# Weight buffers of a streaming encoder layer: high and low parts 64 bytes apart, four buffers at four places modulo 256 bytes

## The chip, the core and the metric

The kernel runs on one core of one Trainium2 chip. The metric is device time in microseconds of the whole program, one launch. Before the change it is 2326.92 us, the median of 3 runs (2326.52 to 2327.61). Experiments further down compare each kernel with the one before the change on the same chip.

## The reference

The reference is one step of a hybrid encoder layer on two sets of frames, 512 of a new stream and 64 of a running one, 576 in all, with 2048 channels, in float32:

```
hn = rmsnorm(x, g_norm1)
q, k, v, gb, gc, hc = split(hn @ w_in)              # 6 x 1024 columns
o_attn = stick_breaking(rmsnorm(q), rmsnorm(k), v)  # 8 heads x 128; the 64 frames also see 512 cached ones
o_conv = gb * conv3(gc * hc)                        # causal, 3 taps
x = x + concat(rmsnorm(o_attn), rmsnorm(o_conv)) @ w_out      # 2048 x 2048
h2 = rmsnorm(x, g_norm2)
x = x + (silu(h2 @ w_gate) * (h2 @ w_up)) @ w_down  # 2048 x 5632, twice, and 5632 x 2048
```

It returns the new x, the new keys and values, and the state of the convolution. Nearly all of the arithmetic is in the five weight matrices w_in, w_out, w_gate, w_up and w_down.

## The kernel before, in words

**Layout.** Channels lie on the 128 partitions, frames on the free axis. The 576 frames are handled as two halves of 288 (HALF). Every product is a series of matmuls in which 128 x 128 weights are loaded into the array and 288 frames are streamed past them.

**Two parts for each number.** A float32 operand is split in two: a high part, which ScalarE makes by a cast to the matmul's format (float32r), and a low part, the rest, which VectorE makes by a subtraction (lines 291 and 292, 228 and 231, 784 and 787, 1484 and 1487). A product then takes three matmuls for each 128 channels: high weights by high frames, low weights by high frames, high weights by low frames. In the text these three are a triple. Weights are split as they arrive from memory; frames are split once and stay in SBUF, high part and low part behind each other in a tile of 2 x 288 numbers, so the low part begins 1,152 bytes behind the high one.

**Units.** Most of the work is done in units of a seven-product scheme (Strassen's, in the form with few sums): a unit has two by two blocks of weights and two by two blocks of frames, seven products instead of eight, numbered 1 to 7 in the code. A product of a gate or up unit has NP = 8 weight blocks of 128 x 128, so 8 x 3 = 24 matmuls, all into one PSUM tile (psy, psw or psx). There are 44 gate and up units and 37 pieces of 8 down units (line 2028), units of the same kind for five pairs of input columns (line 1162), and for the convolution's columns and the attention half of w_out (line 1515). The first columns of w_in and the convolution half of w_out are done without the scheme, by `product` (line 282).

**Weight buffers.** The pool wpool holds one raw tile of 16,384 bytes of each partition (raw_a), into which SyncE's DMAs bring weights, and two tags, whi and wlo, with two buffers each of 8,192 bytes. As the program is laid out, raw_a begins at byte 2,816 of each partition and the four buffers at 19,200, 27,392, 35,584 and 43,776, all of them at 0 modulo 256. The weights of line 282 use one whi and one wlo buffer, high part in the one and low part in the other. A unit's product uses one buffer alone, whl: the tile is [2, NP, 128], its first 4,096 bytes are the high part and the rest the low part, and products take the tags in turn, so that the four buffers go round. The tiles `lpad` (32 bytes, behind wpool, rpool and tmp on the left side) and `rpad` (224 bytes, first on the right) bring the tiles that follow to multiples of 256; streamed frames begin at 0 (high part) or 128 (low part) modulo 256.

**Order.** TensorE's instructions stand in the order in which the code writes them. A unit's products follow a written list (`order`, and `horder` and `corder` in the earlier stages); `prepare` (from line 1981), `unit_prepare` and `conv_prepare` split the weights of a product four places ahead of the one that runs. So a buffer's cast waits until the product that used it before has run, and its contents are needed some three products later. Splitting a gate or up product's weights is one ScalarE cast and one VectorE subtraction of 128 x 1024. VectorE also makes the sums of weight blocks that the seven-product scheme needs, and most of the work behind the products.

Of the kernel before, what the change touches and what calls it, by code (L numbers as in the profile page):

```python
# [11 lines left out]
F32R = mybir.dt.float32r  # L12
# [4 lines left out]
P = 128  # L17
# [17 lines left out]
NP = KD // 2  # L35
# [32 lines left out]
def down_calls():  # L68

    done, calls, gone = [0] * DC, [], 0  # L70
    for d, a, b in DOWN:
        assert done[d] == a and b <= gone + SLOTS
        done[d] = b
        calls.append([p + SLOTS for p in range(gone, min(done)) if p + SLOTS < NFP])
        gone = min(done)
    assert gone == NFP
    return calls


class Pipeline:  # L80


    def __init__(self):
        self.now, self.seq, self.heap = 0, 0, []
# [24 lines left out]
def tile_hybrid_stream_step(  # L109
# [19 lines left out]
    wpool = ctx.enter_context(tc.tile_pool(name="wpool", bufs=2, side="left"))  # L129
# [45 lines left out]
    ready = []  # L175
    raw_tile = {"A": wpool.tile([P, 2, 2048], F32, tag="raw", name="raw_a", bufs=1)}

    def weight_raw(i):
        src, nk, ncol = specs[i]
        raw = raw_tile["A"][:, 0 if len(EARLY) <= i < first_out else i % 2, : nk * ncol]  # L180
        return raw, raw.rearrange("p (k c) -> p k c", k=nk), src

    def weight_split(i):
        nk, ncol = specs[i][1:]
        hi = wpool.tile([P, 2048], F32R, tag="whi", name=f"whi{i}")[:, : nk * ncol]
        lo = wpool.tile([P, 2048], F32R, tag="wlo", name=f"wlo{i}")[:, : nk * ncol]
        ready.append((hi.rearrange("p (k c) -> p k c", k=nk), lo.rearrange("p (k c) -> p k c", k=nk)))
        return hi, lo

# [272 lines left out]
    with tc.manual_schedule(engines={mybir.EngineType.Activation, mybir.EngineType.DVE, mybir.EngineType.SP}):  # L462
        raw, raw3, src = weight_raw(0)
        raws[0] = raw
        hi, lo = weight_split(0)
# [317 lines left out]
    def cast(hi, src):  # L783
        nc.scalar.copy(out=hi, in_=src)

    def low(lo, src, hi):
        nc.vector.tensor_tensor(out=lo, in0=src, in1=hi.bitcast(F32), op=ALU.subtract)
# [314 lines left out]
    bt = {}  # L1102
    hfree, hregion, hst, hoper = [], {}, {}, {}
# [4 lines left out]
    def call_blocks(gone):  # L1108
        hfree.extend(gone)
        while hwanted and hfree:  # L1110
            n, c, s = hwanted.pop(0)
            q = hfree.pop(0)
            v = bt["g"] if q == 4 else raw_tile["A"][:, q // 2, q % 2 * 1024 : (q % 2 + 1) * 1024]
            v = v.rearrange("p (j c) -> p j c", c=P)
            c0 = UNIT_COLS[n][c][0] * AW + UNIT_COLS[n][c][1] * P
            nc.sync.dma_start(out=v, in_=w_in[:, c0 : c0 + P].rearrange("(j s p) c -> s p j c", s=2, p=P)[s])
            hregion[n, c, s] = q, v

    def unit_prepare(n, p_):
        st, tt = hst.setdefault(n, {"gone": []}), nc.vector.tensor_tensor  # L1120
        gone, own = st["gone"], bt["own"]
        first_sum = p_ in (6, 7) and 6 not in gone and 7 not in gone

        def raw(c, s):
            return hregion[n, c, s][1]

        if first_sum:
            tt(out=raw(1, 0), in0=raw(1, 0), in1=raw(0, 0), op=ALU.subtract)
            if p_ == 6:
                tt(out=own, in0=raw(1, 0), in1=raw(1, 1), op=ALU.add)  # L1130
        src = own if p_ in (3, 6) else raw(*{1: (0, 0), 2: (0, 1), 4: (1, 1), 5: (1, 0), 7: (1, 0)}[p_])
        bt["turn"] = bt.get("turn", 0) + 1
        whl = hoper[n, p_] = wpool.tile([P, 2, NP, P], F32R, tag=("whi", "wlo")[bt["turn"] % 2], name="whl")
        cast(whl[:, 0], src)
        if first_sum and p_ == 7:
            tt(out=own, in0=raw(1, 0), in1=raw(1, 1), op=ALU.add)
        yield 2
        low(whl[:, 1], src, whl[:, 0])
        gone.append(p_)
        if p_ in (6, 7) and not first_sum:  # L1140
            yield 1
            tt(out=raw(1, 0), in0=own, in1=raw(0, 0), op=ALU.add)
            tt(out=own, in0=raw(0, 1), in1=own, op=ALU.subtract)
        free = {4: [(1, 1)], 5: [(1, 0)]}.get(p_, [])
        if p_ in (2, 6, 7) and all(q in gone for q in (2, 6, 7)):
            free = [(0, 0), (0, 1)]
        call_blocks([hregion.pop((n, c, s))[0] for c, s in free])
# [144 lines left out]
    for q in (2, 3):  # L1292
        pipe.spawn(unit_prepare(*horder[q]), 3 * (q - 2))
# [134 lines left out]
    cturn = [0]  # L1428
# [26 lines left out]
    def conv_prepare(n, p_):  # L1455

        st, tt, m = cst.setdefault(n, {"left": 7, "gone": []}), nc.vector.tensor_tensor, NP if n < NCU else NH // 2
        gone, early = st["gone"], n < NCU  # L1460
        first_sum = early and p_ in (6, 7) and 6 not in gone and 7 not in gone
        if p_ == 1:
            _, st["a11"], st["a12"] = cregion[n, 0]
            st["at"] = {p: st[s] for p, s in ((1, "a11"), (2, "a12"))}
        at = st["at"]
        if first_sum or not early and p_ == 6:
            _, st["a21"], st["a22"] = cregion[n, 1]
            a11, a12, a21, a22 = (st[s] for s in ("a11", "a12", "a21", "a22"))
            own = bt["s1"] if early else bt["s1"][:, n % 2 * m : (n % 2 + 1) * m]
            at.update({3: own, 4: a22, 5: a21, 6: own, 7: a21} if early else {3: a12, 4: a22, 5: own, 6: a11, 7: a21})  # L1470
            if not early:
                tt(out=own, in0=a21, in1=a22, op=ALU.add)
            tt(out=a21, in0=a21, in1=a11, op=ALU.subtract)
            if not early:
                tt(out=a11, in0=own, in1=a11, op=ALU.subtract)
            elif p_ == 6:
                tt(out=own, in0=a21, in1=a22, op=ALU.add)
        if not early and p_ == 3:
            tt(out=at[3], in0=at[3], in1=at[6], op=ALU.subtract)
        src = at[p_]  # L1480
        cturn[0] += 1
        whl = wpool.tile([P, 2, NP, P], F32R, tag=("whi", "wlo")[cturn[0] % 2], name="whl")[:, :, :m]
        coper[n, p_] = whl
        nc.scalar.copy(out=whl[:, 0], in_=src)
        if first_sum and p_ == 7:
            tt(out=at[6], in0=at[7], in1=at[4], op=ALU.add)
        tt(out=whl[:, 1], in0=src, in1=whl[:, 0].bitcast(F32), op=ALU.subtract)
        gone.append(p_)
        if early and p_ in (6, 7) and not first_sum:
            tt(out=at[5], in0=at[6], in1=st["a11"], op=ALU.add)  # L1490
            tt(out=at[3], in0=st["a12"], in1=at[6], op=ALU.subtract)
        if p_ == 4 or (p_ in (2, 6, 7) and all(q in gone for q in (2, 6, 7)) if early else p_ == 3):
            c = int(p_ == 4)
            q = cregion.pop((n, c))[0]
            if n < NCU or (n, 1 - c) not in cregion:
                call_columns([q])
# [167 lines left out]
    for k_, (n, p_) in enumerate(corder):  # L1664
# [9 lines left out]
        if n == NCU - 1 and p_ in (6, 7, 4):  # L1674
            q = {6: 1, 7: 2, 4: 3}[p_]
            t = bt["pool"].tile([P, NH, 2, HALF], F32R, tag=f"t{q}", name=f"forms{q}")
# [286 lines left out]
    slot_turn = [0]  # L1963
# [17 lines left out]
    def prepare(n, p_):  # L1981

        st = unit.setdefault(n, {"summed": -1})
        m = UNITS[n][3]
        if p_ == 1:
            st["a11"], st["a12"] = (region[n, 0][0][:, :, q, :] for q in range(2))
        if p_ == 7 and n == 0:
            one_sum(n)
            one_sum(n)
        if p_ == 6:  # L1990
            while st["summed"] != 6:
                one_sum(n)
        if p_ == 3:
            while st["summed"] != 3:
                one_sum(n)
        src = {1: "a11", 2: "a12", 3: "a12", 4: "a22", 5: "s1", 6: "a11", 7: "a21"}[p_]
        slot_turn[0] += 1
        whl = wpool.tile([P, 2, NP, P], F32R, tag=("whi", "wlo")[slot_turn[0] % 2], name="whl")[:, :, :m]
        split(whl[:, 0], whl[:, 1], st[src])
        operand[n, p_] = whl  # L2000
        if n >= NGU:

            if p_ == 1:
                summing.append(n)
            if summing and p_ != 2:
                k = summing[0]
                if unit[k]["summed"] != 6 or p_ == 6:
                    one_sum(k)
                if unit[k]["summed"] == 3:
                    summing.pop(0)  # L2010
        if p_ in (3, 4):
            st["gone"] = st.get("gone", 0) + 1
            if n < NGU:
                load_columns(region.pop((n, p_ - 3))[1])
            elif st["gone"] == 2:
                load_columns(region.pop((n, 0))[1])
# [104 lines left out]
    for d, v in visits.items():  # L2121
        n = next(a for a, b in zip(v, v[1:]) if a >= NGU + 10 and b >= a + 4)
# [6 lines left out]
    turn = [0]  # L2129
# [252 lines left out]
```

## Time and profile before

| | |
|---|---|
| median of 3 runs | 2326.92 us |
| the profiled execution | 2329.04 us |
| its span in the profile | 2327.3 us |
| mean granted TensorE clock | 0.999 |
| instructions in the span | 43,744 |
| matmuls, and weight loads | 17,437 each |
| DMA traffic | 402.54 MB, mean 173 GB/s |

The profile is one execution of the program. Times are in microseconds, and ns where it is said. PE is TensorE's matmuls, PEld its weight loads, which overlap them; DVE is VectorE, ACT ScalarE, POOL GpSimd, SP SyncE. Matmuls are pipelined and their ends are modelled, so the length that a row gives for one matmul (some 294 ns) is longer than the distance from one matmul's start to the next; the distance is read from starts, or from a count in a stretch without idle time. The chain is the work that ended last, followed back from the end of the program; a piece of it is a start, a length, an engine, a tile, a line and a count. In a row of a group stand the line, engine, operation, the tile written and the tiles read, partitions x elements and the count; then the busy time, the mean ns of one, and the engine's idle time before them with what ended it.

### The profile page before, as it was taken

The page shows a single profiled execution, that of the slowest core. Times are in us where ns is not written, and L with a number is a line of the kernel's source. Part 1 is how long each engine was busy: PE and PEld are TensorE (multiplying, and loading weights), DVE is VectorE, ACT ScalarE, POOL GpSimd, SP SyncE. Part 2 cuts the span into 40 slices and gives each one's busy share as a digit, 9 for nine tenths or more (in the row PEclk, how much of TensorE's full clock was granted, in tenths as well). Part 3 has the DMA queues.
Part 4 walks back from the last instruction along what each step waited for, and adds up shares of the span by engine and source line. Part 5 has one row for each costly group of instructions (what it writes and reads, how often), then busy time and mean ns, then how long its engine had stood idle before and what let it go on. Part 6 is the DMA issues. An engine that isn't in the chain of part 4 may idle for free.

```text
span 2327.3 us, 43744 instructions
## 1 busy us (share of the span) xinstructions
PE 2317.9 (100%) x17437; PEld 2310.7 (99%) x17437; DVE 1919.4 (82%) x2853; ACT 1161.8 (50%) x2016; POOL 284.8 (12%) x394
## 2 busy tenths in 40 slices
PE   9999999999999999999999999999999999999999
PEld 9999999999999999999999999999999999999999
DVE  8977887888877899888888888888888777887886
ACT  7535887444445564444444444444444444444444
POOL 2002343111111220000000000000000001431121
PEclk9999999999999999999999999999999999999999
DMA  8776564953389454444444444344354936886653
GB/s 277 212 207 169 151 156 107 335 182 117 111 271 238 150 175 145 155 145 134 155 130 149 141 138 154 122 153 151 116 160 138 358 114 219 218 238 198 194 133 103
DMA packets 584869, 402.54 MB, mean 173 GB/s; under 512 B 91870, under 2 KB 571864, under 8 KB 584664
## 3 DMA queue, kind: packets, MB, share of 16 engines
q1 hardware_dynamic: 574136, 378.56, 52.3%
q0 software_dynamic: 10160, 20.94, 4.0%
q8 instruction: 136, 2.23, 0.4%
q14 instruction: 69, 0.57, 0.1%
q10 hardware_dynamic: 368, 0.24, 0.0%
HBM read 303.53 MB, written 96.16 MB: 172 GB/s over the span
## 4 chain that ended last, share of the span: by engine, by line
PE 92%; DVE 3%; DMA 3%; SPq 1%; issue 1%; ACT 0%; ACTq 0%; DVEq 0%
PE psy L2028 36%; PE psw L2028 18%; PE psx L2028 9%; PE psy L1515 6%; PE pj L282 6%; PE pjo L282 4%; PE psw L1515 3%; PE psy L1162 3%; PE psx L1515 2%; PE psw L1162 1%; DMA raw_a<-in_w_in_dram 1%; PE psx L1162 1%; DMA form_dram<-hf 1%; PE po L1048 1%; PE z L920 1%
## 5 line engine op out<-in xcount | busy, mean ns | idle before, releaser
L2028 PE MATMUL psy<-h_s,whl 128*128 128x288 f32 x2787 | 411.3, 294 | 0.0
L2028 PEld LDWEIGHTS psy<-h_s,whl 128*128 128x128 f32 x2787 | 383.4, 188 | 0.0
L292 DVE TENSOR_TENSOR whl<-raw_a,whl 128x1024 fp32r<-128x1024 f32 (+4 forms) x296 | 318.5, 1077 | 57.5 <-ACT whl L291 56.6
L2028 PE MATMUL psw<-t,whl 128*128 128x288 f32 x2400 | 347.7, 295 | 0.0
L2028 PEld LDWEIGHTS psw<-t,whl 128*128 128x128 f32 x2400 | 327.3, 188 | 0.3 <-DVE whl L292 0.2
L291 ACT CAST whl<-raw_a 128x1024 fp32r<-128x1024 f32 (+4 forms) x296 | 268.1, 907 | 103.8 <-issue 35.4
L282 PE MATMUL pj<-x,whi 128*128 128x288 f32 x1248 | 272.7, 299 | 0.0
L292 DVE TENSOR_TENSOR whl<-raw_b,whl 128x1024 fp32r<-128x1024 f32 (+5 forms) x190 | 198.9, 1047 | 65.9 <-ACT whl L291 65.2
L291 ACT CAST whl<-raw_b 128x1024 fp32r<-128x1024 f32 (+5 forms) x190 | 165.5, 872 | 165.8 <-issue 72.6
L2038 ACT COPY part<-psy 128x288 f32<-128x288 f32 x242 | 96.4, 398 | 279.2 <-PE psy L2028 278.2
L282 PEld LDWEIGHTS pj<-x,whi 128*128 128x128 f32 x1248 | 207.5, 189 | 0.5
L282 PE MATMUL pj<-x,wlo 128*128 128x288 f32 x624 | 184.2, 295 | 0.0
L2028 PE MATMUL psy<-b22m,whl 128*128 128x288 f32 x1212 | 183.0, 294 | 0.0
L2028 PE MATMUL psy<-t2t,whl 128*128 128x288 f32 x1212 | 182.6, 294 | 0.0
L2028 PE MATMUL psx<-h_s,whl 128*128 128x288 f32 x1185 | 173.1, 294 | 0.0
L2028 PEld LDWEIGHTS psy<-t2t,whl 128*128 128x128 f32 x1212 | 168.0, 188 | 0.2 <-DVE whl L292 0.2
L2028 PEld LDWEIGHTS psy<-b22m,whl 128*128 128x128 f32 x1212 | 167.9, 188 | 0.0
L2028 PEld LDWEIGHTS psx<-h_s,whl 128*128 128x128 f32 x1185 | 162.5, 188 | 0.0
L291 ACT CAST whl<-s 128x1024 fp32r<-128x1024 f32 (+5 forms) x81 | 72.2, 892 | 100.8 <-PE psw L2028 100.7
L1807 POOL DMA_DIRECT2D hid_dram<-form x3 | 2.3, 752 | 971.6 <-DVE form L292 970.1
L282 PEld LDWEIGHTS pj<-x,wlo 128*128 128x128 f32 x624 | 117.4, 188 | 0.3
L2028 PE MATMUL psy<-t,whl 128*128 128x288 f32 x576 | 106.7, 295 | 0.0
(535 smaller groups left out, 4555.4 us busy)
## 6 DMA issues: line engine op xcount, KB each, us to landing
hid_dram<-form SPq DMA_DIRECT2D x147, 288.0 KB, 2.2
raw_a<-in_w_in_dram SPq DMA_DIRECT2D x31, 1024.0 KB, 5.5
raw_a<-in_w_gate_dram SPq DMA_DIRECT2D x22, 1024.0 KB, 5.7
raw_a<-in_w_up_dram SPq DMA_DIRECT2D x22, 1024.0 KB, 5.7
raw_b<-in_w_gate_dram SPq DMA_DIRECT2D x22, 1024.0 KB, 6.5
raw_b<-in_w_up_dram SPq DMA_DIRECT2D x22, 1024.0 KB, 6.4
h_s<-hid_dram SPq DMA_DIRECT2D x10, 2016.0 KB, 12.2
raw_a<-in_w_out_dram SPq DMA_DIRECT2D x16, 1024.0 KB, 5.5
```

The costliest lines, as they stand in the source:

```text
L282: mm(ps, w_[:, k, csl], x_, start=(k == 0 and n == 0), stop=(k == nk - 1 and n == 2))
L291: nc.scalar.copy(out=hi, in_=src)
L292: (lo_eng or nc.vector).tensor_tensor(out=lo, in0=src, in1=hi.bitcast(F32), op=ALU.subtract)
L920: mm(zb(i), w[a_][:, kk], w[b_][:, q0:TP], start=(n == 0), stop=False, skip_group_check=True)
L1048: mm(w["po"][:, i * P : 512], w[a_][:, i, :], w[f"{b_}{i}"][:, : (512, 384, 256)[i]], stop=(i == 0 and n == 2), **kw)
L1162: mm(ps, whl[:, w_, j, :], x_, start=(start and j == 0 and q == 0), stop=(j == NP - 1 and q == 2), skip_group_check=True)
L1515: mm(ps, whl[:, w_, j, :], x_, start=(start and j == 0 and q == 0), stop=(j == m - 1 and q == 2), skip_group_check=True)
L1807: q.dma_start(out=hid_dram[fp][2 * n - 2 : 2 * n].rearrange("f p t -> p f t"), in_=t.bitcast(F32))
L2028: mm(ps, whl[:, w_, j, :], x_, start=(start and j == 0 and q == 0), stop=(j == len(xs_) - 1 and q == 2), skip_group_check=True)
L2038: nc.scalar.copy(out=t, in_=st["y"])
```

## The change

The buffers of both tags grow from 2,048 to 2,064 numbers (8,256 bytes, 32 x 256 + 64). Four of them behind each other begin at 0, 64, 128 and 192 modulo 256 bytes, and what lies behind them on the left side moves by 256 bytes. A unit's weights now stand in such a buffer with the low part first, at its beginning, and the high part at number 1,040, that is 64 bytes behind the low part's end; high and low parts are 64 apart modulo 256. The class TwoParts lets the rest of the code index the two parts as before. The weights of line 282 keep their two buffers, each cut to its first 2,048 numbers. No instruction is added, taken away or moved.

```
+class TwoParts:
+
+    def __init__(self, hi, lo):
+        self.two = (hi, lo)
+
+    def __getitem__(self, key):
+        part, rest = key[1], (key[0], *key[2:])
+        if isinstance(part, slice):
+            return TwoParts(*(t[rest] for t in self.two[part]))
+        return self.two[part][rest]
...
+    def weight_tile(tag, name):
+        return wpool.tile([P, 2064], F32R, tag=tag, name=name)[:, :2048]
+
+    def unit_weights(turn):
+        t = wpool.tile([P, 2064], F32R, tag=("whi", "wlo")[turn % 2], name="whl")
+        return TwoParts(*(t[:, a : a + 1024].rearrange("p (j c) -> p j c", c=P) for a in (1040, 0)))
...
-        hi = wpool.tile([P, 2048], F32R, tag="whi", name=f"whi{i}")[:, : nk * ncol]
-        lo = wpool.tile([P, 2048], F32R, tag="wlo", name=f"wlo{i}")[:, : nk * ncol]
+        hi = weight_tile("whi", f"whi{i}")[:, : nk * ncol]
+        lo = weight_tile("wlo", f"wlo{i}")[:, : nk * ncol]
...
-        whl = hoper[n, p_] = wpool.tile([P, 2, NP, P], F32R, tag=("whi", "wlo")[bt["turn"] % 2], name="whl")
+        whl = hoper[n, p_] = unit_weights(bt["turn"])
...
-        whl = wpool.tile([P, 2, NP, P], F32R, tag=("whi", "wlo")[cturn[0] % 2], name="whl")[:, :, :m]
+        whl = unit_weights(cturn[0])[:, :, :m]
...
-        whl = wpool.tile([P, 2, NP, P], F32R, tag=("whi", "wlo")[slot_turn[0] % 2], name="whl")[:, :, :m]
+        whl = unit_weights(slot_turn[0])[:, :, :m]
```

## The prediction

> **What bounds the kernel now.** I read the page first (busy times, granted clock, the chain's shares), then the chain in order of time, then TensorE's own waits, then the groups by form, and last TensorE's timeline where its operands change names. The page:
>
> ```profile
> span 2327.3 us, 43744 instructions
> PE 2317.9 (100%) x17437; PEld 2310.7 (99%) x17437; DVE 1919.4 (82%) x2853; ACT 1161.8 (50%) x2016; POOL 284.8 (12%) x394
> PEclk9999999999999999999999999999999999999999
> PE 92%; DVE 3%; DMA 3%; SPq 1%; issue 1%; ACT 0%; ACTq 0%; DVEq 0%
> ```
>
> TensorE is never idle and its granted clock is full; 92% of the chain that ended last is its matmuls. The time is a number of matmuls times the spacing of one. The chain in order of time gives that spacing:
>
> ```profile
> 749.49 101.55 PE pjo L282 x768
> 887.13 9.52 PE psy L2028 x72
> 909.34 9.52 PE psy L2028 x72
> ...
> 1775.66 9.52 PE psy L2028 x72
> ```
>
> ```profile
> 1198.12 9.52 PE psy L2028 x72
> 1207.64 3.17 PE psw L2028 x24
> 1210.81 3.17 PE psx L2028 x24
> ...
> 1220.33 9.52 PE psy L2028 x72
> ```
>
> A gate or up unit is seven products of 24 matmuls, 168 in all. The first pieces of two units stand 909.34 - 887.13 = 22.21 us apart, and 1775.66 - 887.13 = 888.53 us is exactly 40 units: 888.53 / (40 x 168) = 0.13222 us, so **132.2 ns for each matmul**. The output projection of the convolution half, which keeps high and low weights in two separate buffers, gives 101.55 / 768 = 132.2 ns. The pace is the same at every place, though ScalarE, VectorE and DMA beside it do different things: it is set inside TensorE. Counted from the loops, 2,688 matmuls of line 282, 11,088 of line 2028 and 3,024 of lines 1162 and 1515 read a buffer that the change moves: **16,800**, or 16,800 x 132.2 ns = 2,221 us of the 2,327.3 us span. 0.2% (about what a measurement of this kernel can tell from no change) is 4.7 us, or 0.28 ns of one matmul.
>
> **The change, part by part.** It adds, removes and reorders no instruction. The same four buffers of the same two tags take turns, the same ScalarE cast and VectorE subtraction fill them, and as many DMAs are issued; none of them touches these buffers. Only addresses differ. Four edits have to be priced.
>
> *Pads.* Four buffers of 8,256 bytes (32 x 256 + 64) in place of 8,192 push everything behind them on the left side by 4 x 64 = 256 bytes, a whole turn of 256, so no other tile's place modulo 256 changes. Cost 0.
>
> *The fills.* Today the cast reads a raw column that begins at 0 modulo 256 (raw_a at byte 2816) and writes the high part, also at 0; the subtraction reads both and writes the low part at 0. After the change the high part stands 64 bytes off the low one. If standing alike hurt these two engines today, their time per element would show it:
>
> ```profile
> L292 DVE TENSOR_TENSOR whl<-raw_a,whl 128x1024 fp32r<-128x1024 f32 x176 | 215.0, 1222 | 18.9 <-ACT whl L291 18.7
> L1487 DVE TENSOR_TENSOR whl<-raw_a,whl 128x512 fp32r<-128x512 f32 x48 | 32.6, 690 | 7.8 <-ACT whl L1484 7.5
> L291 ACT CAST whl<-raw_a 128x1024 fp32r<-128x1024 f32 x176 | 185.2, 1053 | 50.2 <-issue 35.4 <-PE psx L2028 11.3 <-DVE raw_a L1976 2.1
> L1484 ACT CAST whl<-raw_a 128x512 fp32r<-128x512 f32 x48 | 29.7, 621 | 14.3 <-DMA raw_a<-in_w_out_dram 5.6 <-PE psw L1515 4.7 <-PE psx L1515 2.7
> ```
>
> VectorE takes (1222 - 690) / 512 = 1.04 ns per further element, ScalarE (1053 - 621) / 512 = 0.84 ns. No row shows either of them at another residue, so the fill may go either way. What hides it: TensorE hardly ever waits for a weight.
>
> ```profile
> PE psw L1515 <- ACT whl L1484: 1.0, 1, 1.0
> PE psw L1515 <- DVE whl L1487: 0.9, 1, 0.9
> PE psy L1515 <- DVE whl L1487: 0.2, 1, 0.2
> PE psy L1162 <- DVE whl L787: 0.2, 1, 0.2
> ```
>
> That is 2.3 us in the whole span, so faster fills can give back at most 2.3 us. Slower ones cost nothing while they are covered: VectorE's share of the 40 units is
>
> ```profile
> 887.13:1775.66 888.53, 888.53 (x6722) 888.53 (x6722) 749.70 (x1023) 413.05 (x620) 0.00 (x0) 1.00 0.45 142
> ```
>
> 749.70 of 888.53 us, of which the 40 x 7 subtractions are 280 x 1.222 = 342 us. The cover is gone when these grow by the 138.8 us that VectorE has left, some 40%; from there, each further 1% would cost 3.4 us in this stretch. I take 0.
>
> *The weight reads.* Each matmul is preceded by a load of 128 columns, 512 bytes of each partition, read while the matmul before it still streams 288 columns, 1,152 bytes. Today every such load begins at 0 modulo 256. The streamed parts begin at 0 (high half, used by the first two matmuls of a triple) or at 128 (low half: 1,152 = 4 x 256 + 128). So the two readers stand 0 apart in two matmuls of three and 128 apart in the third. After the change the low weights begin at r and the high ones at r + 64, with r going through 0, 64, 128, 192 from product to product: all four distances come equally often, and half of the matmuls have one, 64 or 192, that this trace never shows. What does distance cost? The nearest rows are the attention products, whose operands all begin at multiples of 256 (every step is 512 bytes or a whole number of them), against the 288-column ones with a third of them 128 off:
>
> ```profile
> L1048 PE MATMUL po<-ph,vh 128*128 128x512 f32 x8 | 3.2, 395 | 0.0
> L1048 PE MATMUL po<-ph,vl 128*128 128x512 f32 x8 | 3.1, 394 | 0.0
> L1048 PE MATMUL po<-pl,vh 128*128 128x512 f32 x8 | 3.1, 389 | 0.0
> L1048 PE MATMUL po<-ph,vh 128*128 128x256 f32 x8 | 2.2, 280 | 0.0
> L1048 PE MATMUL po<-ph,vl 128*128 128x256 f32 x8 | 2.2, 279 | 0.0
> L1048 PE MATMUL po<-pl,vh 128*128 128x256 f32 x8 | 2.2, 278 | 0.0
> L2028 PE MATMUL psw<-t,whl 128*128 128x288 f32 x2400 | 347.7, 295 | 0.0
> ```
>
> The mean is 392.7 ns for 512 columns and 279.0 ns for 256, so 113.7 / 256 = 0.444 ns per column. At 288 columns the line gives 279.0 + 32 x 0.444 = 293.2 ns; the row has 295. Standing 128 off in one matmul of three therefore costs no more than 1.8 ns, if anything. The same slope bounds the gain: 288 x 0.444 = 127.9 of the 132.2 ns go with the streamed columns, and only 4.3 ns can belong to a load of constant size. 16,800 x 4.3 ns = 72 us, so no better than 2,255.
>
> The other bound comes from a beat in TensorE's own timeline, in the down units, where the streamed tile changes name at each triple (high x high, low x high, high x low):
>
> ```profile
> 2103.91 0.55 PE L2028 MATMUL psy<-t2t,whl 128*128 128x288 f32 x3
> 2104.31 0.56 PE L2028 MATMUL psy<-t,whl 128*128 128x288 f32 x3
> 2104.70 0.56 PE L2028 MATMUL psy<-h_s,whl 128*128 128x288 f32 x3
> 2105.11 0.56 PE L2028 MATMUL psy<-b22m,whl 128*128 128x288 f32 x3
> 2105.50 0.55 PE L2028 MATMUL psy<-t,whl 128*128 128x288 f32 x3
> 2105.89 0.56 PE L2028 MATMUL psy<-h_s,whl 128*128 128x288 f32 x3
> 2106.29 0.56 PE L2028 MATMUL psw<-t2t,whl 128*128 128x288 f32 x3
> 2106.69 0.56 PE L2028 MATMUL psw<-t,whl 128*128 128x288 f32 x3
> 2107.09 0.55 PE L2028 MATMUL psw<-h_s,whl 128*128 128x288 f32 x3
> 2107.48 0.56 PE L2028 MATMUL psw<-b22m,whl 128*128 128x288 f32 x3
> ```
>
> Triples start 0.40, 0.39, 0.41, 0.39, then 0.39, 0.40, 0.40, 0.40 us apart: single ones differ (the view rounds to 0.01), four together take 1.59 us both times. The beat runs on when tile and product change, so it is not the address of a tile; but something inside TensorE makes equal work take 0.39 to 0.41 us, and it repeats with the present, always equal, places of the weights. If the new places put every triple at the quick pace, that is 3 x 132.2 - 390 = 6.7 ns on each of 5,600 triples, 37 us; at the slow pace, 13.3 ns, 75 us more. These are the two ends, 2,290 and 2,402. I take 0 between them, by the row it is nearest to: the 288-column row, where a shift of half the period moved a matmul by at most 1.8 ns and the trace shows no stall to take away.
>
> A rule of the Trainium skill speaks against any effect. SBUF — State Buffer, "Who interferes with whom", gives TensorE two read ports, one for the moving operand and one for the weight load, independent of each other and shared with no engine. By that rule the sum is 0 and the time 2,326.9; the constant 132.2 ns beside changing neighbours agrees, and no row here has the two readers at 64 or 192.
>
> The sum: 0 + 0 + 0 + 0. The profiled execution took 2,329.04 us, 1.7 us around its span and 2.1 us (0.09%) above the median of 2,326.92. With nothing to add, the forecast is that median, **2,326.9 us**.
>
> **The rivals.** *The two readers do meet (faster).* Today's equal places make the load and the stream collide, and 64 bytes apart they miss each other. For it: the beat, and up to 4.3 ns per matmul that no column accounts for. Against it: a distance of 128 shows no gain. Price: down to 2,290 if all triples run at the quick pace, half of that 2,308. A second rule belongs beside this rival: TensorE: Matmul & The Clock Gate, "Back-to-back issue gap", has columns / 2.4 + 2.5 ns, an estimated 122.5 ns for 288; by it 9.7 ns of each matmul, 163 us in all, is stall. The 0.444 ns per column of the attention rows disagrees with it.
>
> *The new distances are the bad ones (slower).* At 64 or 192 the load and the stream enter the same part of the memory together, at the matmuls of lines 2028, 1162, 1515 and 282. For it: half of all matmuls get a distance never seen here. Against it: 128 is harmless. Price: with one of the two bad, a quarter of the triples at 0.41 us, 5,600 / 4 x 13.3 ns = 18.6 us, 2,345.5; with both, 2,364; above +0.28 ns per matmul on the mean it decides.
>
> *The buffers don't stand where the words say.* If the allocator rounds 8,256 up to a larger step, only the 64 bytes between high and low remain. The price lies inside the two above; I count it with no change.
>
> **How the numbers follow.** No change: 0.42, as three of the four edits are covered and the fourth has one harmless neighbour, but half of its cases lie outside the trace. The readers meet: 0.36, of which 0.30 between 2,290 and 2,322 and 0.06 below. Bad distances: 0.20, of which 0.12 up to 2,346 and 0.08 above; fills that lose their cover: 0.02, counted as above 2,346. The range 2,290 to 2,346 leaves out 0.16. The likeliest case alone spans 2,322.3 to 2,331.6. Faster 0.36, same 0.42, slower 0.22.
>
> **What would show it.** Right: units 22.21 us apart, pieces of 24 matmuls at 3.17, the same beat of 1.59 us for four triples, cast and subtraction at 1053 and 1222 ns, still some 2 us of waits for weights. Rival one: pieces of 24 below 3.16, quicker or no beat. Rival two: pieces above 3.18, by a different amount in each of the four buffers. The prediction is wrong if 40 units take less than 886.7 or more than 890.3 us.

## The result

The changed kernel takes 2323.26 us (median of 20 runs, 2319.34 to 2326.66), the kernel before on the same chip 2327.57 us (20 runs, 2325.83 to 2330.93): a ratio of 0.9979, 95% interval 0.9972 to 0.9986. That is 0.21% faster, 4.3 us, just at the bound of what a measurement can tell from no change. The forecast of 2,326.9 us was near, and its reason, that the place of the weights makes no difference, was wrong: the pace is now different in each buffer, and the differences nearly cancel. So its nearness is luck.

The page of the changed kernel, whose line numbers are 19 higher:

```profile
span 2320.7 us, 43744 instructions
PE 2310.6 (100%) x17437; PEld 2302.8 (99%) x17437; DVE 1919.7 (83%) x2853; ACT 1161.1 (50%) x2016; POOL 285.3 (12%) x394
PEclk9999999999999999999999999999999999999999
```

As many matmuls, the same full clock, the same busy time on the other engines. TensorE is still the bound, and its busy time is 7.3 us shorter. The chain in order of time (start, length, engine, tile, line, count), in the stretches shown of before:

```profile
882.81 9.47 PE psy L2047 x72
904.94 9.51 PE psy L2047 x72
...
1202.48 3.15 PE psw L2047 x24
1205.63 3.15 PE psx L2047 x24
1208.78 3.19 PE psy L2047 x24
1211.97 3.17 PE psw L2047 x24
1215.14 9.48 PE psy L2047 x72
1224.63 3.17 PE psw L2047 x24
1227.80 3.15 PE psx L2047 x24
...
1769.01 9.47 PE psy L2047 x72
```

Before, each product of 24 matmuls took 3.17 us. Now four lengths go round, 3.15, 3.15, 3.19, 3.17: one for each buffer. In the order of use the pairs of places (begin of the high part, begin of the low part, modulo 256) are (192, 128), (64, 0), (0, 192), (128, 64). The four add up to 12.66 us where they were 4 x 3.173 = 12.69. From the first pieces of the units, 40 units now take 1769.01 - 882.81 = 886.20 us, or 131.9 ns per matmul, where they took 888.53 us and 132.2 ns. By 16,800 matmuls the difference of 0.35 ns is 5.8 us, of 6.6 us between the two spans. The weights of line 282, in two buffers, stand at (0, 128) or (64, 192), since the tag wlo begins 128 bytes on; in the output projection their paces are 3.186 and 3.148, with a mean of 3.167. The fills did not move, as the groups by form show (mean ns of one behind the busy time):

```profile
L311 DVE TENSOR_TENSOR whl<-raw_a,whl 128x1024 fp32r<-128x1024 f32 x176 | 215.2, 1223 | 18.1 <-ACT whl L310 17.9
L310 ACT CAST whl<-raw_a 128x1024 fp32r<-128x1024 f32 x176 | 184.9, 1052 | 49.6 <-issue 35.3 <-PE psx L2047 11.0 <-DVE raw_a L1995 2.1
```

TensorE's waits for weights, 2.3 us before, are 0.5 us (engine, tile, line, what it waited for; us, times, longest):

```profile
PE psy L1534 <- DVE whl L1506: 0.3, 1, 0.3
...
PE psy L1181 <- DVE whl L806: 0.2, 1, 0.2
```

So nearly the whole effect is a change of pace inside TensorE, from product to product.

### The profile page after: what moved, and what is told of

Its sections match the earlier page's. It is cut to its first block, busy times and chain, and to the rows that moved or that the text cites. A ratio compares the mean times of both kernels' runs of the same rounds, so it can differ in the third digit from the quotient of the medians.

```text
span 2320.7 us, 43744 instructions
## 1 busy us (share of the span) xinstructions
PE 2310.6 (100%) x17437; PEld 2302.8 (99%) x17437; DVE 1919.7 (83%) x2853; ACT 1161.1 (50%) x2016; POOL 285.3 (12%) x394
## 4 chain that ended last, share of the span: by engine, by line
PE 88%; DVE 6%; DMA 2%; SPq 2%; issue 1%; ACT 1%; POOL 0%; ACTq 0%; DVEq 0%
PE psy L2047 34%; PE psw L2047 17%; PE psx L2047 8%; PE pj L301 8%; PE psy L1534 7%; PE psw L1534 3%; PE psy L1181 3%; PE psx L1534 2%; PE psw L1181 1%; PE psx L1181 1%; DMA raw_a<-in_w_in_dram 1%; SPq L2244 1%; DMA raw_b<-in_w_down_dram 1%; DVE whl L311 1%; DVE wlo L211 1%
```

## Experiments

Three theories stood at the beginning. *Place theory*: a product's pace is set by where its two weight parts stand modulo 256, seen from the streamed frames. *Gap theory*: the 64 bytes between high and low part do it. *Neighbour theory*: what counts is that successive products use different buffers. In what follows a pair (h, l) is the place of the high and of the low weights modulo 256 bytes, with the frames at 0 (high) and 128 (low) where nothing else is said, and a pace is us per product of 24 matmuls.

### Pads alone, and the parts in the other order

In the first kernel the buffers begin at 0, 64, 128 and 192, with high and low part behind each other as before; in the second the gap of 64 bytes is there, with the high part first.

```
-        return TwoParts(*(... for a in (1040, 0)))
+        return TwoParts(*(... for a in (0, 1024)))      # pads alone
+        return TwoParts(*(... for a in (0, 1040)))      # high part first
```

Expected of pads alone: 

> The four buffers begin at 0, 64, 128 and 192 modulo 256 as after the change, but high and low weights of a unit lie behind each other, both at the same place. Place theory (the pace of a product is set by where its two weight parts begin against the streamed frames, modulo 256 bytes): the products of the four buffers take different times again, the buffer at 0 keeps 3.17 us for 24 matmuls, the other three differ from it by 0.01 to 0.04 us; total between 2315 and 2345 us. Gap theory (only that high and low lie apart counts): all 24-matmul pieces at 3.17 us, 2327.6 us, ratio 1.000. Neighbour theory (only that the buffer being filled and the buffer being read lie at different places counts): the whole gain stays, 2323 us, ratio 0.998, and all pieces are alike at 3.16 to 3.17.

Expected of the high part first: 

> As after the change, but the high part stands first in each buffer and the low part 64 bytes behind it, so (high, low) is (0,64), (64,128), (128,192), (192,0) in place of (64,0), (128,64), (192,128), (0,192). Place theory: four paces again, not the same four as after the change (3.15, 3.17, 3.15, 3.19); total between 2310 and 2345 us. Gap theory and neighbour theory: as after the change, 2323 us, ratio 0.998.

Measured, against 2326.67 us for the kernel before (25 runs): pads alone 2331.63 us, ratio 1.0022 (1.0013 to 1.0031); high part first 2331.65 us, ratio 1.0023 (1.0013 to 1.0032). The chain of pads alone:

```profile
1208.01 3.14 PE psw L2047 x24
1211.15 3.20 PE psx L2047 x24
1214.36 3.20 PE psy L2047 x24
1217.56 3.18 PE psw L2047 x24
```

and of the high part first:

```profile
1228.49 3.18 PE psw L2047 x24
1231.67 3.18 PE psx L2047 x24
1234.85 3.18 PE psy L2047 x24
1238.03 3.20 PE psw L2047 x24
```

The second kernel has the gap and the four different buffers of the change, and is slower than before: the gap theory and the neighbour theory both fall. The place theory holds as far as each pair has its own pace: the four pieces shown of pads alone belong, in order, to (128, 128), (0, 0), (192, 192) and (64, 64). But (0, 0) is the pair of the kernel before, where it takes 3.173. Here it comes behind (128, 128), the quickest, and takes 3.204 (mean of the distances between starts). So the place isn't all.

### The frames moved by 64 bytes, the weights left alone

```
-    lpad.tile([P, 8], F32, name="lpad_t")
+    lpad.tile([P, 24], F32, name="lpad_t")
-    small = rpad.tile([P, 56], F32, name="rpad_t")
+    small = rpad.tile([P, 104], F32, name="rpad_t")
```

> The kernel before, weights all at 0 modulo 256, but both pads grow so that every streamed tile begins 64 bytes further on (64 and 192 in place of 0 and 128). Place theory, if only the distance counts: all products alike, at the pace that the buffer at 192 has in the kernel with pads only, to 0.01 us in 24 matmuls. If the absolute place counts: another common pace. Gap theory and neighbour theory: 3.17 us, 2327.6 us, ratio 1.000.

Measured: 2342.37 us, ratio 1.0068 (1.0051 to 1.0085). Its chain:

```profile
1201.08 9.60 PE psy L2028 x72
1210.68 3.20 PE psw L2028 x24
1213.88 3.20 PE psx L2028 x24
```

No weight was moved, and every product takes 3.20, the pace of (192, 192) in pads alone: there too the weights stand 192 above the high frames, or 64 below them. That fits a rule by the distance between the two, and not by where either stands by itself. The filling of the weight buffers is not the cause here, since none of them moved.

### Two quick pairs and (0, 0) twice

The buffers of one tag get the low part first and the gap, those of the other none, so that products go round (64, 0), (0, 0), (192, 128), (0, 0).

```
+    SIZE = {"whi": 2048, "wlo": 2080}
...
+        two = (1040, 0) if tag == "wlo" else (0, 1024)
```

> The two buffers of tag wlo begin at 0 and 128 and hold the low part first and the high part 64 bytes behind it, which are the two quick cases after the change; the two of tag whi stay at 0 with no gap, as before. Place theory: 24-matmul pieces alternate 3.15 and 3.17 us, a mean of 131.7 ns for a matmul, 16,800 x 0.5 ns = 8.6 us less than before, 2319 us, ratio 0.9963. Gap theory: half of the effect of the change, 2325.5 us, ratio 0.999. Neighbour theory: less than the change brings, since three buffers begin at 0: 2325 us or more.

Measured: 2329.36 us, ratio 1.0012 (1.0003 to 1.0021), where the place theory had about 2319. Its chain:

```profile
1229.11 3.20 PE psw L2051 x24
1232.30 3.15 PE psx L2051 x24
1235.45 3.18 PE psy L2051 x24
1238.63 3.19 PE psw L2051 x24
```

(64, 0) keeps its 3.15. But (192, 128), which took 3.15 in the changed kernel, takes 3.19 here, and (0, 0) takes 3.175 behind (64, 0) and 3.197 behind (192, 128). Paces found in one order of products can't simply be added up for another. That gave the next theory its name: a product's pace also hangs on what it inherits from the product before it (*carry theory*).

### The frames moved by 128 and by 192 bytes

The same edit as for 64 bytes, with `lpad` of 40 and `rpad` of 88 numbers for 128, 56 and 72 for 192. Every product is the same, so nothing can be inherited from a different one.

Expected for 128: 

> The kernel before with every frame moved on by 128 bytes and no weight buffer moved: the hi frames then lie 128 and the lo frames 0 above the weights, modulo 256, in every product. Place theory (a product's pace is set by the distance, modulo 256, between the bytes of its weights and those of its frames): this is the case that the buffer at 128 had in the run with pads alone, 3.142 us for 24 matmuls against 3.173 before, so 700 products x 31 ns = 22 us less: about 2305 us, with pieces of 24 at 3.14 all through. Carry theory (a product's pace hangs as much on the product before it, and 3.142 came only after the products of the other buffers): the steady pace of a uniform sequence may be anything between the fastest and slowest pieces met so far, 3.14 to 3.20, so 2304 to 2346 us; a time above 2318 would speak for it.

Expected for 192: 

> The kernel before with every frame moved on by 192 bytes and no weight buffer moved; the distance is that of the buffer at 64 in the run with pads alone. Place theory: 3.179 us per 24 matmuls, 700 x 6 ns = 4 us more than before, about 2331 us. Carry theory: anything between 2304 and 2346 us, with one steady pace of pieces all through.

Measured, against 2327.83 us: by 128 2326.08 us, ratio 0.9990 (0.9977 to 1.0004), its single runs from 2318.48 to 2331.0; by 192 2332.94 us, ratio 1.0020 (1.0010 to 1.0031). The first missed the place theory's 2305 by 21 us. Its chain, at two places:

```profile
115.32 3.14 PE psw L1162 x24
118.47 3.15 PE psx L1162 x24
121.61 3.15 PE psy L1162 x24
...
1204.08 3.17 PE psw L2028 x24
1207.25 3.17 PE psx L2028 x24
1210.42 3.17 PE psy L2028 x24
```

The places, and so the distances, are the same in both. At 115 us the pace is 3.147, at 1204 us 3.173. Between the starts of triples, taken 100 us at a time, the mean is 3.15 from 100 to 200 us, 3.173 from 500 to 700, between the two from 700 to 900, and 3.173 from 900 to 2200. The granted clock is 1.00 in all of these. So this distance has two steady paces. The kernel falls from one into the other where something breaks the row of triples. One such place lies inside line 1515, with the same tiles before and behind it (the chain, then TensorE's timeline):

```profile
468.80 3.15 PE psy L1515 x24
...
500.96 3.17 PE psw L1515 x24
```

```profile
491.31 9.66 PE L1515 MATMUL psy<-x,whl 128*128 128x288 f32 x71 [0.36 <-DVE whl L1487]
```

Up to 490.66 us the pace is 3.146; TensorE then waits 0.36 us for a weight, and from there it is 3.173. Near 743 us it goes back to 3.147 at single matmuls of another kind (line 598), without a wait. The single runs lie 12.5 us apart, and 700 products at the one pace or the other would differ by some 18 us; that the two paces are the reason was not shown, since one execution alone has a trace. By 192 the pace is 3.18, as (64, 64) in pads alone, with stretches of 3.173.

### A survey of pairs

To get each pair's pace without neighbours, the four buffers were laid in one tile: all high parts behind each other, all low parts behind each other, 256 bytes of slack between and around, and a new pair every 19 products.

```
+    wall = wpool.tile([P, 8256], F32R, tag="w", name="wall", bufs=1)
+    def starts(h, l):
+        if l >= h or l == 0:
+            return h, 4096 + (l if l >= h else 64)
+        return 4096 + h, l
...
+        h, l = starts(16 * (made[0] // 19 % 16 // 4), 16 * (made[0] // 19 % 4))
```

Expected with steps of 64 bytes: 

> The changed kernel with the four buffers laid in one tile whose hi parts and lo parts can begin at any of 0, 64, 128 and 192 modulo 256; every 19 products the pair (hi, lo) goes to the next of the 16, and each product of a stretch has the same pair. The computation is that of the reference. It is run for the pace of each pair in a steady stretch, not for its total. Place theory: (0, 0) 3.173 us per 24 matmuls, (64, 64) 3.18, (128, 128) 3.14, (192, 192) 3.20, and the pairs of the changed kernel near what they took there: (64, 0) 3.15, (192, 128) 3.15, (128, 64) 3.18, (0, 192) 3.19. Carry theory: each stretch settles to one pace, but for the pairs that were only met among others it differs from those values by 10 ns or more, up or down.

Expected with steps of 32 bytes: 

> The one tile with pairs (hi, lo) at odd multiples of 32 bytes, a new pair of 16 every 19 products, for the pace of each pair and not for its total. Where the pair changes, a slot can overlap its old neighbour, so some products there read weights that are partly overwritten. Place theory with a grain of 64 bytes: (32, 0) is as (0, 0) or (64, 0), (96, 0) as (64, 0) or (128, 0), (160, 0) as (128, 0) or (192, 0) and so on, each on one of 3.147, 3.173, 3.18, 3.19, 3.20 and 3.227. With a grain of 32 bytes or finer, some pairs lie off these, perhaps below 3.14.

In these two, and in the three kernels with one tile and one pair below, a slot is in places written anew before its last reading, so part of the new x comes from other weights than the reference's (for the first survey this departs from its expectation). The number and order of TensorE's matmuls are the same; only their pace is read. The surveys took 2457.02 and 2461.68 us, since where pairs change a slot overlaps its old neighbour and has to wait. Two stretches in TensorE's timeline of the first, (192, 64) and then (64, 0), each with two products that start 72 matmuls apart:

```profile
1231.69 3.39 PE L2061 MATMUL psw<-t,wall 128*128 128x288 f32 x24
...
1241.37 3.39 PE L2061 MATMUL psw<-t,wall 128*128 128x288 f32 x24
...
1703.33 3.31 PE L2061 MATMUL psw<-t,wall 128*128 128x288 f32 x24
...
1712.77 3.31 PE L2061 MATMUL psw<-t,wall 128*128 128x288 f32 x24
```

9.68 us for 72 matmuls is 3.227 for 24; 9.44 is 3.147. The granted clock is 1.00 in both, so it is not a slower clock. A third pace lies between them, that of (96, 0) in the second survey, whose pieces start 3.20 us apart:

```profile
582.88 3.36 PE L1551 MATMUL psw<-xs_t,wall 128*128 128x288 f32 x24
586.08 3.36 PE L1551 MATMUL psx<-x,wall 128*128 128x288 f32 x24
```

The paces of all 31 pairs, from the mean distance between the starts of triples in the stretch, without those in which TensorE waited; a stretch came once to three times, and two values are two stretches:

| pace, us per 24 | pairs (high, low) |
|---|---|
| 3.147 to 3.151 | (32, 0), (64, 0), (64, 32), (64, 192), (128, 96), (128, 128), (224, 0) |
| 3.147 or 3.20 | (64, 128), (192, 128) |
| 3.164 to 3.181 | (0, 0), (0, 64), (64, 64), (64, 96), (64, 224), (96, 32), (128, 64) |
| 3.182 to 3.189 | (0, 128), (0, 192), (32, 224), (192, 0) |
| 3.20 | (32, 64), (64, 160), (96, 0), (96, 64), (128, 0), (128, 192), (160, 0), (192, 192), (192, 224) |
| 3.211 | (160, 32) |
| 3.227 | (192, 64) |

The steady paces are not spread evenly. Most sit on 3.147, 3.173, 3.200 and 3.227, steps of 0.027 us, and some between two of them (3.182 to 3.189, 3.211). No pair is steadily quicker than 3.147. For the changed kernel's four pairs the survey gives 3.147 (or 3.20), 3.147, 3.186 and 3.173, in sum 12.65 with the lower value and 12.71 with the other, and 12.66 was measured: there the additive reading works, if the lower value is taken. A grain of 64 bytes fails: (224, 0) has 3.147, where its neighbours (192, 0) and (0, 0) have 3.182 and 3.173 or more.

### One pair for the whole kernel

The one tile with a fixed pair, in three kernels: the pair of before as a control, a quick pair, and the slowest.

```
+        h, l = starts(0, 0)       # or starts(16, 0), or starts(48, 16), in numbers of 4 bytes
```

Expected of (0, 0): 

> The same one tile with hi and lo parts at 0 modulo 256, as in the kernel before: it sets the cost of the one tile by itself. Place theory: 2327 us, as before, within 4 us either way, since a uniform (0, 0) took 3.173 and sometimes 3.18. If one tile costs waits by itself: over 2332, and the runs with other pairs must be read against this one.

Expected of (64, 0): 

> The four weight buffers in one tile, hi parts of all of them beginning 64 bytes above a multiple of 256 and lo parts at a multiple of 256; the frames where they were before. Every product is then the case (hi 64, lo 0), which settled to 3.147 us per 24 matmuls in each of its three stretches of the survey. Place theory, by steady paces: 700 products x (3.147 - 3.173) us = 18 us less than before, about 2309 us, with all pieces of 24 at 3.15. Carry theory (the survey's stretches of 19 products were too short, and the pace falls back to 3.17 as the frames moved by 128 did): 2320 to 2327 us. A theory that the one tile itself costs waits: over 2330.

Expected of (192, 64): 

> The same one tile with hi parts at 192 and lo parts at 64 modulo 256, the slowest pair of the survey: 3.226 us per 24 matmuls in both of its full stretches. Place theory: 700 x (3.226 - 3.173) = 37 us more than before, about 2364 us. Carry theory: 2330 to 2345 us. If the place of the weights did nothing, 2327.

Measured, against 2327.44 us: (0, 0) 2339.41 us, ratio 1.0052 (1.0036 to 1.0067); (64, 0) 2322.64 us, ratio 0.9979 (0.9970 to 0.9987); (192, 64) 2363.28 us, ratio 1.0153 (1.0132 to 1.0173). The one tile itself costs 12 us. None of it is pace: the control has 3.173 all through, as the kernel before. The undisturbed distances between starts add up to the same as before, so it lies in waits and what follows on them; the two longest waits of the control, behind a piece of its chain, are not there in the kernel before:

```profile
1199.68 3.17 PE psx L2061 x24
```

```profile
PE pj L315 <- DVE wall L1520: 2.9, 1, 2.9
PE pj L315 <- ACT wall L1517: 2.6, 1, 2.6
```

Against the control, (64, 0) gains 16.8 us and (192, 64) loses 23.9; the pace in the trace of (64, 0) is 3.15 in every product:

```profile
1210.60 3.15 PE psw L2061 x24
1213.75 3.15 PE psx L2061 x24
```

The slow pair came out at 2363.28 as forecast, but by two errors that cancel: the forecast left out the 12 us of the tile and took 3.227 for the whole run. Its trace has 3.227 from 500 to 700 us and 3.200 from 900 on, both at a granted clock of 1.00, so this distance also has two paces. Here too waits change it: within the output projection it is 3.200 before and 3.227 behind a wait of 0.5 us near 846 us, and 3.200 again behind one of 1.70 us at 871 us. The single runs lie 12.6 us apart (2355.14 to 2367.74), and the trace is that of the quickest.

### The quick pair without the one tile

Eight buffers of 1,024 numbers, four for high parts at 64 and four for low parts at 0 modulo 256, each freed by itself; an early weight of line 282 takes two of each. The computation is the reference's.

```
+    def half_tile(tag, name):
+        t = wpool.tile([P, 1024], F32R, tag=tag, name=name, bufs=4)
+        if tag == "hi" and not pads:
+            pads.append(wpool.tile([P, 48], F32, tag="pad1", name="pad1", bufs=1))
+        return t
+    wpool.tile([P, 16], F32, tag="pad0", name="pad0", bufs=1)
```

> Eight buffers of 1024 columns in place of the four of 2048, four for hi parts at 64 and four for lo parts at 0 modulo 256, each freed by itself, so that the waits of the one tile (12 us, from the run with hi and lo at 0) need not come; an early weight takes two buffers of each kind. Every product is the case (64, 0). Place theory: about 700 products x (3.147 - 3.173) us = 18 us less than before, about 2309 us, with all pieces of 24 at 3.15; the one tile's own step from (0, 0) to (64, 0) was 16.8 us, which gives 2311. If part of those 12 us came from the place of the weights and not from the one tile: 2315 to 2323 us.

Measured: 2315.32 us (5 runs, 2312.46 to 2316.33) against 2326.81 us: ratio 0.9942, interval 0.9929 to 0.9956. It is quicker than both kernels. Its page and its chain:

```profile
span 2314.3 us, 43747 instructions
PE 2301.9 (99%) x17437; PEld 2292.9 (99%) x17437; DVE 1917.9 (83%) x2853; ACT 1161.2 (50%) x2016; POOL 281.1 (12%) x394
```

```profile
1204.10 3.15 PE psw L2074 x24
1207.24 3.15 PE psx L2074 x24
```

The time is at the lower edge of the case that put part of the 12 us down to the place of the weights, but that is not the reason: the pace is what was expected, 3.147 all through, 700 x 0.026 = 18 us, and 11.5 us arrive. TensorE is 99% busy now, with waits that the kernel before does not show at this size, such as

```profile
PE psx L472 <- DMA xin<-in_x_prompt_dram: 2.1, 2, 1.8
PE ss L644 <- ACT b22m L337: 2.0, 1, 2.0
```

The two traces, laid beside each other matmul by matmul, show where the rest is. The undisturbed distances between starts add up to 19.7 us less than before, and 6.7 us come back elsewhere: 5.3 of them around the second of these waits and 3.1 in the first 30 us, with smaller gains and losses besides. Behind that wait the first 21 matmuls take 5.24 us, where the next 21 take 2.92:

```profile
855.46 5.24 PE L2074 MATMUL psy<-h_s,whl 128*128 128x288 f32 x21
...
860.95 2.92 PE L2074 MATMUL psx<-h_s,whl 128*128 128x288 f32 x21
```

The granted clock is 0.92 from 855 to 890 us, and 1.00 in the kernel before from 855 to 900. So the wait and the slower matmuls behind it make up the 5.3 us. Why the wait is there was not followed up.

## Why the prediction was right in size and wrong in mechanism

*What bounds the kernel*: right. The time followed the spacing of TensorE's matmuls, but for the waits that one tile (12 us, and more in the surveys) and eight buffers (some 7 us) added.

*Pads and fills, cost 0*: right. 1223 and 1052 ns stand against 1222 and 1053, and waits for weights fell from 2.3 to 0.5 us. VectorE's and ScalarE's times show nothing of the 64 bytes.

*The weight reads, "I take 0"*: this step failed. It went by the 288-column row, "where a shift of half the period moved a matmul by at most 1.8 ns and the trace shows no stall to take away". That row holds one combination only, the one of before, and says that this one costs no more than 1.8 ns above a line; it can't say what the others do. Its numbers are also lengths with modelled ends, not spacings: over the kernels here the same attention rows of 512 columns read 388 to 397 ns, and the 288-column row 294, 295 and 296 where the spacing is 131.1, 132.2 and 133.3. What stood in the place of 0 is a spacing that depends on the pair of places. The runs showed four levels: 131.1, 132.2, 133.3 and 134.4 ns for one matmul, a step of 1.1 ns each, with the kernel of before on the second. 1.8 ns was called harmless, and the whole effect of the change is 0.35 ns per matmul. Against 16,800 matmuls and a bound of 0.28 ns, a limit of 1.8 ns shows nothing. By the same reasoning the high part first (+0.23%), the frames moved by 64 bytes (+0.68%) and the eight buffers (-0.58%) would have come out at 0 too; that the change itself came so near is the luck of four paces that nearly cancel. A smaller slip: the prediction took the places r and r + 64 for all 16,800 matmuls, but the 2,688 of line 282 have parts that stand 128 apart.

*The two ends, 2,290 and 2,402, from the beat*: they hold. The best steady triple is 3.147 / 8 = 0.393 us where 0.390 was taken, the worst 3.227 / 8 = 0.403 where 0.410 was taken. But the beat by itself is no sign of a collision: the quick pair has one too, with triples of 390 and 397 ns in turn in the kernel with eight buffers (near 1200 us), and (192, 64) at 3.200 has none, with triples of 400.

*The rule of two read ports* (the Trainium skill, SBUF — State Buffer, "Who interferes with whom"), by which, as the prediction reads it, the place could do nothing: the runs disagree with that reading, since moving the frames by 64 bytes, and no weight, cost 0.68%. Whether the two ports disturb each other is not shown. *The rule of the issue gap* (the Trainium skill, TensorE: Matmul & The Clock Gate, "Back-to-back issue gap"), an estimated 122.5 ns: the Trainium skill gives that formula for a single matmul by itself and says that a stream with weight loads is spaced otherwise. No pair of the survey came below 131.1.

*The rivals*: a sign of each of the first two came, in the same kernel. "Pieces of 24 below 3.16" are there in two buffers, and a piece above 3.18 in one of the four. The mechanism of the two, that load and stream meet, is not shown by that. The third, that the buffers don't stand where the words say, falls: four paces go round, as four places would have it. The fault in the reasoning was to set a single sign for all four distances. Two buffers gain 0.024 each, one loses 0.014 and one 0.004 (3.149, 3.148, 3.187 and 3.177 against 3.173): 0.03 us for four products, which leaves the 0.2%. The prediction's own mark, 40 units below 886.7 us, was passed with 886.20.

What stays open: why these distances have these paces. No simple rule was found in the table (a pair and its neighbour 32 bytes away can lie two steps apart), and that the weight load and the stream meet in some part of the memory was argued, not shown. What makes a distance with two paces fall into one or the other wasn't settled either; the traces only show that it changes at a wait of TensorE, at matmuls of another kind, or behind another pair. The 128 bytes between high and low frames were never varied.

## What to carry to other kernels

A kernel that TensorE bounds to 100% has one more quantity to look at: the length of equal pieces in the chain, to the third digit. If the same count of matmuls takes different times, or a shift of one operand by 32 or 64 bytes changes it, the distance of weights and streamed data modulo 256 bytes is worth a survey: give all products one quick distance that has held its pace in every stretch, since different ones in turn cancel and disturb each other. And a bound from a nearby row is of use only if it is finer than the effect per instruction that would decide: here 1.8 ns against 0.28.

## What the runs showed of the hardware

In a product of three matmuls to a weight block, the spacing of the 288-column matmuls depends on the distance, modulo 256 bytes, between weights and streamed data in SBUF. (In the kernel before, frames in tiles 2,304 = 9 x 256 bytes long stand odd and even multiples of 256 from the weights, all at 3.173.) Steady paces sit mostly on 3.147, 3.173, 3.200 and 3.227 us per 24 matmuls; the slowest is 2.5% above the quickest. Some distances have two steady paces, and a kernel can go from one to the other within an execution, with nothing moved: 3.146 up to a wait of 0.36 us at 491 us, and 3.173 behind it.
